# Decoder block with a mixture of experts, one core: half of the experts take 64 tokens, with both weight-side parts of a token in one stationary operand

## The chip, the cores and the metric

One NeuronCore of a Trainium2 chip runs the whole kernel. The metric is the time of one execution in device microseconds (us); the time of a kernel is the median of its runs. TensorE is called PE, VectorE DVE, ScalarE ACT, GpSimd POOL and SyncE SP, as in the profile. A profile comes from one profiled execution, and its span is the time from that execution's first recorded event to its last.

## What is computed

The reference is one decoder layer on 512 tokens of 1024 channels, in float32: a modulated norm, an attention and a delta-rule mixer, a residual, a second modulated norm, and a mixture of experts, of which the change speaks alone:

```python
logits = (xt @ w_router + b_router).astype(jnp.float32)
top_v, top_e = lax.top_k(logits, TOP_K)
gates = jax.nn.softmax(top_v, axis=-1)
...
def clamped_swiglu(hgu):
    gate, up = jnp.split(hgu, 2, axis=-1)
    gate = jnp.minimum(gate, SWIGLU_LIMIT)
    up = jnp.clip(up, -SWIGLU_LIMIT, SWIGLU_LIMIT)
    return gate * jax.nn.sigmoid(SWIGLU_ALPHA * gate) * (up + 1)
...
def expert_block(args):
    xb, e = args
    return clamped_swiglu(xb @ w1[e] + b1[e]) @ w2[e] + b2[e]
```

`w1[e]` is 1024 x 2048 (8 MB), `w2[e]` 1024 x 1024 (4 MB); the output is the residual plus the gated sum of a token's four experts, then a final norm. With the reference's inputs the 32 experts get 20 to 175 tokens: experts 0 and 1 get 23 and 104, the two fullest of the others 175 and 134, the next thirteen 114 to 55, and the last fifteen 49 to 20.

## The kernel before, in words

The first 440 us (mixer, out-projection, router) are not touched. From there the kernel goes through the experts one after the other, 0 to 31 in an order that is made at run time (L1295 to L1324): experts 0 and 1 first, and the two with most tokens at the places H0 = 8 and H1 = 20, where a second list of 128 tokens follows the first. Every other expert has one list of 128 places. A list names the tokens (`idx`) and their gates (`gate`); places that no token fills name a row past the end of the tokens.

A list passes through these steps.
- POOL gathers the tokens' rows from DRAM (`gather`, L1136, tile `xg`). PE transposes them in 8 pieces into PSUM (`transposed`, L1121, tile `tr`); ACT casts them to the fast matmul type float32r (`xH`) and DVE subtracts that from the exact value, which gives the rest (`xL`). A product of two such split numbers takes three matmuls: high by high, high by low, low by high.
- SP loads the weights in tiles of 1 MB (`raw`, twelve in flight). `halves` (L1018) splits half a tile: ACT casts it to `wh` (L1026), and DVE or POOL makes `wl = raw - wh` (L1028). `wh` and `wl` have NS = 4 buffers each, so a split is at most four halves ahead of PE. An expert has 24 halves, 16 of `w1` and 8 of `w2`; a counter over all halves (`hseq`) gives every 12th to POOL (L1027), that is 2 of an expert's 24.
- `up` (L1141): the bias enters PSUM by four matmuls (L1052), and 16 halves follow with six matmuls of 512 columns each (L1151, L1152, L1155). Then ACT computes the Silu (`sg`, L1159), DVE the clamp (L1161, out of PSUM) and the product (L1165).
- `down` (L1168): the result is transposed and split again (`aH`, `aL`), and 8 halves follow with six matmuls each (L1185, L1186, L1189). DVE multiplies by the gate (`y`, L1197), and POOL adds the 128 rows to `yd` in DRAM (L1198); empty places add to spare rows of `yd`.

The steps stand in the order up(i), down(i-1), up(i+1), down(i) (L1372). The transposes are hung in between the tiles of a down projection (`pending`). A scheduler orders each engine's instructions from there; every engine then executes its own in that order. The lists of four experts at a time are made by comparisons on DVE (`oh`, L1091). Rounds that the lists do not hold run in a loop at the end (L1481), as many times as there are such rounds.

```python
1026         S.copy(h, t)
1027         on_g = hseq[0] <= 2 or hseq[0] % 12 == 0 and hseq[0] < 24 * E - 24
1028         sub = (G if on_g else V).tensor_tensor(l, t, h.bitcast(F32), op=OP.subtract)
```

Of the kernel before, what the change touches and what calls it, by code (L numbers as in the profile page):

```python
# [29 lines left out]
Z0, DK0, DQ0, DV0 = 3072, 2048, 1536, 2560  # L30


@with_exitstack
def tile_block(ctx: ExitStack, tc, x, c, w_ada, b_ada, norm1_w, w_in, conv_w, A_log, dt_bias, dn_norm_w,
# [109 lines left out]
    # gates first, every token at once, and the first two heads' keys: their products follow the making of h,  # L144
    # two blocks of channels at a time as the modulation of these is known
# [5 lines left out]
    def modulation(k0, n):  # L151
        """shift1 and scale1 of n blocks of channels; these blocks of h."""
# [64 lines left out]
    def k_split(k):  # L217
        """The lower parts for two blocks."""
# [142 lines left out]
    # every unit of weights is read and split one ahead of its use  # L361
# [6 lines left out]
    def take(n):  # L368
        """The next unit; n pieces of the sums above beside it."""
# [6 lines left out]
    def head(kind, h, wu):  # L376
        """One head's channels: convolution; its tokens on partitions; back to channels. A step per yield."""
# [141 lines left out]
    # (not before the projections are nearly done: the tensor engine goes on with what comes first)  # L519
# [54 lines left out]
    def delta():  # L574
# [121 lines left out]
    def item(p, b, po):  # L696
        """Two heads' queries of a block of tokens; the sums over the keys leave by channel."""
# [53 lines left out]
    def router():  # L751
        """logits = (x1 @ (a2 * w_router)) / rms(x1) + shift2 @ w_router + b_router"""
# [20 lines left out]
    def merge(*gens):  # L773
        """Streams of emission, each with its number of steps, advanced in proportion."""
# [19 lines left out]
    E, H0, H1 = 32, 8, 20  # L794
# [31 lines left out]
    yd = dram.tile([T + P, D], F32, name="yd")  # L826
# [12 lines left out]
    # expert biases: parts of float32r, of b1 on (half, part, expert), of b2 on (part, expert) with the first part again;  # L839
    # 1 comes to the upper half of b1, ALPHA and gate2 to b2  # L840
# [33 lines left out]
    def route_half(b, half, between=lambda: None):  # L874
        """Half of the sum of the squares and of the products with the router."""
# [27 lines left out]
    def top4(b, between=lambda: None):  # L903
# [8 lines left out]
        # top 4 of 32, gates, members  # L912
# [8 lines left out]
    def store(b):  # L921
# [6 lines left out]
        if b == 0:  # L928
            S.dma_start(yd[T:T + P, :], x1b)
# [11 lines left out]
    def place(dst, mk, pp):  # L941
        """Place of every token in the lists; 1024 and more where it is no member."""
# [43 lines left out]
    def init_rec(r):  # L986
        """Tokens as pairs of small numbers, membership, gates."""
# [25 lines left out]
    moe = ctx.enter_context(tc.tile_pool(name="moe", bufs=1, reuse_waits="tile"))  # L1013
    prefetch(NL + 4)
# [3 lines left out]
    def halves(t, j, pin=False):  # L1018
        """The two parts of half of a tile of weights."""
# [23 lines left out]
    def accumulators(n, bsel):  # L1043
        """Of the gate and up projections of one or two lists of tokens, with the biases."""
# [5 lines left out]
        for ac in accs:  # L1050
            for n in range(4):
                PE.matmul(ac[n], bsel(n // 2), b1s[:, (n % 2) * 512:(n % 2) * 512 + 512], start=True, stop=False)  # L1052
# [20 lines left out]
    def gate_parts(r, g):  # L1073
        """A gate as three parts of bfloat16."""
# [5 lines left out]
    def fill_lists(n, pos_of, rec_of, ix, go, gates=None):  # L1080
        """Tokens and gates of n lists; gates: makes these in between."""
        ohs, sl = {}, moe.tile([P, n, 6], F32, name="sl")
        for c0, c1 in ((0, 3), (3, 6)) if gates else ((0, 6),):
# [3 lines left out]
            for i in range(n):  # L1087
                if c0 == 0:
                    oh = ohs[i] = moe.tile([P, NTB, P], BF16, name="oh", bufs=2)
                    for b in range(NTB):  # L1090
                        V.tensor_scalar(oh[:, b], iotaS, pos_of(i, b), None, op0=OP.is_equal)  # L1091
# [10 lines left out]
    # experts 0 and 1 come first: their lists  # L1102
# [11 lines left out]
    i8 = moe.tile([P, 8], U32, name="i8")  # L1114
    ev = moe.tile([P, 2, 3, E], F32, name="ev")
# [5 lines left out]
    def transposed(src, name):  # L1121
# [14 lines left out]
    def gather(e, ix, t):  # L1136
        G.indirect_dma_start(out=t, out_offset=None, in_=h2d,  # L1137
                             in_offset=bass.IndirectOffsetOnAxis(ap=ix, axis=0), bounds_check=T - 1, oob_is_err=False)
        XG[e] = t

    def up(sets, tiles, bsel):  # L1141
        """Gate and up projections of one or two lists of tokens of an expert; clamped SwiGLU."""
        xs = [XT.pop(e) for e, _ in sets]
        pu, p2, accs = ACC.pop() if ACC else accumulators(len(sets), bsel)
        for k, t in enumerate(tiles):
            for j in range(2):
                h, l = PRE.pop(0) if PRE else halves(t, j)
                for (xh, xl), ac in zip(xs, accs):
# [4 lines left out]
                    for n in range(2):  # L1153
                        ns = slice(n * 512, n * 512 + 512)
                        PE.matmul(ac[2 * j + n], xl[:, k], h[:, ns], start=False, stop=(k == KT - 1))  # L1155
        for (e, ut), ac in reversed(list(zip(sets, accs))):
# [11 lines left out]
    def down(sets, tiles, between=lambda i: None, last=False, first=False):  # L1168
        """Down projection, gates, and the sum into the rows of the tokens; sets: key, gates, rows."""
        as_ = [AT.pop(e) for e, _, _ in sets]  # L1170
        if first:
# [6 lines left out]
        for i, t in enumerate(tiles):  # L1178
            for j in range(2):
                h, l = halves(t, j, last and i > 0)  # L1180
                k = 2 * i + j
                for (ah, al), py in zip(as_, accs):
# [7 lines left out]
            if i < 3:  # L1190
                between(i)
        for (_, gcol, ix), py in reversed(list(zip(sets, accs))):
            y = moe.tile([P, D], F32, name="y", bufs=2)
            if last:
                add_rows(y, py, gcol, ix, first)
                continue
            lastv[:] = [V.scalar_tensor_tensor(y, flat(py), gcol, gate2, op0=OP.mult, op1=OP.mult).ins]  # L1197
            G.indirect_dma_start(out=yd, out_offset=bass.IndirectOffsetOnAxis(ap=ix, axis=0), in_=y, in_offset=None,  # L1198
                                 bounds_check=T + P - 1, oob_is_err=True, compute_op=OP.add)

# [1 line left out]
    RES = {}  # L1202

    def residual():
        """What is summed so far, and a place for the result."""
# [9 lines left out]
    def gates_by_expert():  # L1215
        """The parts of the gates: the first twice, the second."""
# [11 lines left out]
    def bias2(pn, b, n):  # L1228
        """The sum of the gates and rows of b2 for half of the channels."""
        PE.matmul(pn, RES["g"][:, b * P:b * P + P], b2s[:96, n * 512:n * 512 + 512], start=True, stop=False)  # L1230

    def add_rows(y, py, gcol, ix, first):
        """Rows of an expert onto the rows of their tokens, by products with zeros and ones; the final norm."""
# [25 lines left out]
        def rms(b, xs):  # L1259
            """The sum of the squares of a block, in one part or two; the scale of its rows."""  # L1260
# [30 lines left out]
    # the first gather goes before the other weights  # L1291
# [7 lines left out]
    r, t, i0, i1, t1, cw = (oe_[:, i] for i in range(6))  # L1299
    m8, hf = oe_[:, 6, 0:8], oe_[:, 7, 0:2]  # L1300
    V.tensor_tensor(cw, pc, tieb, op=OP.add)
    V.max(out=m8, in_=cw)
    V.max_index(out=i8, in_max=m8, in_values=cw)
    V.tensor_copy(hf, i8[:, 0:2])
    V.tensor_scalar(i0, iotaE, hf[:, 0:1], None, op0=OP.is_equal)
    V.tensor_scalar(i1, iotaE, hf[:, 1:2], None, op0=OP.is_equal)
    V.tensor_scalar(t, iotaE, hf[:, 0:1], None, op0=OP.is_gt)
    V.scalar_tensor_tensor(t, iotaE, hf[:, 1:2], t, op0=OP.is_gt, op1=OP.add)
    V.tensor_tensor(r, iotaE, t, op=OP.subtract)
    for h in (H0, H1):  # L1310
        V.scalar_tensor_tensor(r, r, h - 0.5, r, op0=OP.is_gt, op1=OP.add)
    for h, i in ((H0, i0), (H1, i1)):
# [220 lines left out]
```

## Time and profile before

| | |
|---|---|
| time, median of 3 runs | 1752.71 us (1749.81 to 1755.13) |
| the profiled execution, its span | 1756.8 us |
| PE busy in the span | 1636.7 us, 93% |
| DVE busy in the span | 1480.4 us, 84% |
| ACT busy in the span | 1090.4 us, 62% |
| POOL busy in the span | 484.0 us, 28% |
| DMA, mean over the span | 280 GB/s, 491.53 MB |

A busy share is an average over the whole span; the part before 440 us has other limits than the experts. In the timeline a row is a run of like instructions of one engine: start, time to the end of the last, engine, line, operation, output and inputs, how many, and in brackets how long the engine was idle before and who released it. Matmuls are pipelined, so a row of one lasts longer (0.39 us) than the distance to the next (0.23 us).

### The profile page before, as it was taken

The page shows a single profiled execution, that of the slowest core. Times are in us where ns is not written, and L with a number is a line of the kernel's source. Part 1 is how long each engine was busy: PE and PEld are TensorE (multiplying, and loading weights), DVE is VectorE, ACT ScalarE, POOL GpSimd, SP SyncE. Part 2 cuts the span into 40 slices and gives each one's busy share as a digit, 9 for nine tenths or more (in the row PEclk, how much of TensorE's full clock was granted, in tenths as well). Part 3 has the DMA queues.
Part 4 walks back from the last instruction along what each step waited for, and adds up shares of the span by engine and source line. Part 5 has one row for each costly group of instructions (what it writes and reads, how often), then busy time and mean ns, then how long its engine had stood idle before and what let it go on. Part 6 is the DMA issues. An engine that isn't in the chain of part 4 may idle for free.

```text
span 1756.8 us, 23357 instructions
## 1 busy us (share of the span) xinstructions
PE 1636.7 (93%) x8154; PEld 1333.3 (76%) x8154; DVE 1480.4 (84%) x1784; ACT 1090.4 (62%) x1384; POOL 484.0 (28%) x334
## 2 busy tenths in 40 slices
PE   4988989999899999999999999999999999999996
PEld 4767777798687777787777777777777777777774
DVE  6678844667999999949799999999687999999997
ACT  4653223632577777737577677777465777777774
POOL 3426961114232222112123322222122322222111
PEclk7999996999899999999999999999999999999998
DMA  8454551063889999968799999999777999999973
GB/s 267 144 168 139 193 168 49 1 237 154 311 309 337 362 375 374 335 226 299 261 353 365 333 341 356 354 380 352 250 252 273 333 361 369 350 365 342 362 285 109
DMA packets 120409, 491.53 MB, mean 280 GB/s; under 512 B 12727, under 2 KB 40031, under 8 KB 87520
## 3 DMA queue, kind: packets, MB, share of 16 engines
q1 hardware_dynamic: 108528, 459.24, 68.7%
q0 software_dynamic: 10432, 28.06, 7.6%
q10 hardware_dynamic: 1328, 2.70, 0.4%
q8 instruction: 65, 1.06, 0.2%
q14 instruction: 56, 0.46, 0.1%
HBM read 474.32 MB, written 24.65 MB: 284 GB/s over the span
## 4 chain that ended last, share of the span: by engine, by line
PE 58%; DVE 17%; DMA 8%; POOL 6%; issue 6%; ACT 4%; SPq 0%; ACTq 0%; DVEq 0%; POOLq 0%
PE up L1152 10%; PE up L1155 10%; PE up L1151 10%; DVE wl L1028 6%; DMA raw<-in_w 6%; PE py L1185 3%; PE py L1189 3%; PE py L1186 3%; PE tr L1129 2%; POOL blk L496 2%; POOL blk L494 2%; PE up L1052 1%; DVE ut L1161 1%; DVE oh L1091 1%; ACT wh L1026 1%
## 5 line engine op out<-in xcount | busy, mean ns | idle before, releaser
L1026 ACT CAST wh<-raw 128x1024 fp32r<-128x1024 f32 x768 | 802.1, 1051 | 365.2 <-PE up L1155 166.5
L1028 DVE TENSOR_TENSOR wl<-raw,wh 128x1024 fp32r<-128x1024 f32 x705 | 860.9, 1259 | 110.5 <-ACT wh L1026 89.9
L1152 PE MATMUL up<-wl,xH 128*128 128x512 f32 x1024 | 403.2, 394 | 9.5 <-POOL wl L1028 4.9
L1151 PE MATMUL up<-wh,xH 128*128 128x512 f32 x1024 | 401.5, 392 | 0.0
L1155 PE MATMUL up<-wh,xL 128*128 128x512 f32 x1024 | 317.7, 391 | 0.0
L1028 POOL TENSOR_TENSOR wl<-raw,wh 128x1024 fp32r<-128x1024 f32 x63 | 156.7, 2488 | 529.9 <-ACT wh L1026 409.0
L1152 PEld LDWEIGHTS up<-wl,xH 128*128 128x128 f32 x1024 | 193.3, 189 | 58.4 <-DVE wl L1028 10.7
L1155 PEld LDWEIGHTS up<-wh,xL 128*128 128x128 f32 x1024 | 193.0, 189 | 40.7
L1151 PEld LDWEIGHTS up<-wh,xH 128*128 128x128 f32 x1024 | 193.6, 189 | 39.7
L1185 PE MATMUL py<-wh,aH 128*128 128x512 f32 x496 | 203.0, 409 | 0.0
L1186 PE MATMUL py<-wl,aH 128*128 128x512 f32 x496 | 197.0, 397 | 0.0
L1198 POOL DMA_INDIRECT yd<-y,idx x33 | 83.2, 2522 | 343.7 <-ACT wh L1026 168.7
L1189 PE MATMUL py<-wh,aL 128*128 128x512 f32 x496 | 158.2, 398 | 0.0
L1189 PEld LDWEIGHTS py<-wh,aL 128*128 128x128 f32 x496 | 92.8, 188 | 21.4
L1186 PEld LDWEIGHTS py<-wl,aH 128*128 128x128 f32 x496 | 93.5, 188 | 19.0
L1185 PEld LDWEIGHTS py<-wh,aH 128*128 128x128 f32 x496 | 93.5, 188 | 18.6
L1165 DVE SCALAR_TENSOR_TENSOR ut<-sg,ut 128x1024 f32<-128x1024 f32 x32 | 81.6, 2551 | 0.7
L1137 POOL DMA_INDIRECT xg<-h2d,idx x33 | 53.1, 1610 | 76.0 <-PE tr L1129 34.7
L133 ACT CAST wH<-raw 128x1024 fp32r<-128x1024 f32 (+1 forms) x34 | 34.4, 1053 | 54.6 <-DMA raw<-in_w_in 21.2
L354 DVE SCALAR_TENSOR_TENSOR macc<-raw,cond,macc 128x512 f32<-128x512 f32 x62 | 57.0, 959 | 7.9 <-DMA raw<-in_w_ada 7.9
L282 PE MATMUL mm<-hH,wH 128*128 128x512 f32 x144 | 58.6, 407 | 3.5 <-ACT cu L308 1.7
L1129 PE MATMUL tr<-ident,ut 128*128 128x128 f32 x256 | 39.4, 284 | 21.6 <-DVE xL L1131 18.9
(452 smaller groups left out, 2350.3 us busy)
## 6 DMA issues: line engine op xcount, KB each, us to landing
raw<-in_w SPq DMA_DIRECT2D x384, 1024.0 KB, 7.9
raw<-in_w_ada SPq DMA_DIRECT2D x16, 1024.0 KB, 5.0
raw<-in_w_in SPq DMA_DIRECT2D x12, 1024.0 KB, 8.5
raw<-in_w_ada SPq DMA_DIRECT2D x16, 512.0 KB, 9.3
raw<-in_w_out SPq DMA_DIRECT2D x4, 1024.0 KB, 7.8
raw<-in_w_in SPq DMA_DIRECT2D x2, 1040.0 KB
xn<-in_x SPq DMA_DIRECT2D x4, 512.0 KB, 3.9
x<-in_x SPq DMA_DIRECT2D x4, 512.0 KB
```

What stands on the lines that cost most here:

```text
L282: PE.matmul(ps, wh[:, k, js], hH[:, k], start=(k == 0), stop=False)
L1026: S.copy(h, t)
L1028: sub = (G if on_g else V).tensor_tensor(l, t, h.bitcast(F32), op=OP.subtract)
L1129: tc.keep_in_program_order(PE.transpose(pt[:, i], src[:, k * P:(k + 1) * P], ident))
L1151: PE.matmul(ac[2 * j + n], xh[:, k], h[:, ns], start=False, stop=False)
L1152: PE.matmul(ac[2 * j + n], xh[:, k], l[:, ns], start=False, stop=False)
L1155: PE.matmul(ac[2 * j + n], xl[:, k], h[:, ns], start=False, stop=(k == KT - 1))
L1165: lastv[:] = [V.scalar_tensor_tensor(ut, sg, GATE_MAX, ut, op0=OP.min, op1=OP.mult).ins]
L1185: PE.matmul(py[:, n], ah[:, k], h[:, ns], start=(k == 0), stop=False)
L1186: PE.matmul(py[:, n], ah[:, k], l[:, ns], start=False, stop=False)
L1189: PE.matmul(py[:, n], al[:, k], h[:, ns], start=False, stop=(k == KT - 1))
L1198: G.indirect_dma_start(out=yd, out_offset=bass.IndirectOffsetOnAxis(ap=ix, axis=0), in_=y, in_offset=None, bounds_check=T + P - 1, oob_is_ ...
```

## The change

1. The order of the experts is by their number of tokens. The two fullest of experts 2 to 31 go to places 8 and 20, the next thirteen to the even places, the last fifteen to the odd places 3 to 31 (`SMALL`); experts 0 and 1 stay at places 0 and 1. The order is made by comparing every expert with every other on DVE.
2. A list at an odd place holds 64 tokens. Its stationary operand (`hl`) has the high parts of the 64 tokens in columns 0 to 63 and the low parts in columns 64 to 127, so that one matmul with `wh` and one with `wl` give all products, the low parts' in PSUM rows 64 to 127: four matmuls for each half in place of six (`up_small`, and `short` in `down`).
3. The two groups of rows have to be added. ACT copies rows 64 to 127 out of PSUM (`lo`, `ylo`), and matmuls with a 64 x 64 identity add them to rows 0 to 63 (`fold`): four for an up projection, hung into the next down projection, and two for a down projection, after the first tile of the next up projection. Clamp, product and `y` of such a list wait for the fold. The last expert's rows need no fold.
4. Every 4th half of the weights goes to POOL, from half 25 to 743: 6 of an expert's 24 in place of 2.
5. Empty places are no longer scattered: their row is out of bounds and dropped. Gather and scatter of a list of 64 take 64 rows.

Two places in the instruction order. First POOL, in the stretch of ordinary experts after place 20; `wl` is the lower part of half a tile of weights, `xg` the gathered rows, `yd` the sums in DRAM. Before:

```order
L1137 DMA xg_3919<-h2d,idx 128x1024
L1198 DMA yd<-y,idx 640x1024
L1028 TENSOR_TENSOR wl<-raw,wh 128x1024 x2
L1137 DMA xg_3920<-h2d,idx 128x1024
L1198 DMA yd<-y,idx 640x1024
L1028 TENSOR_TENSOR wl<-raw,wh 128x1024 x2
```

And after the change, in the same stretch:

```order
L1158 DMA xg_3924<-h2d,idx 64x1024
L1036 TENSOR_TENSOR wl<-raw,wh 128x1024 x2
L1277 DMA yd<-y,idx 512x1024
L1036 TENSOR_TENSOR wl<-raw,wh 128x1024 x4
L1158 DMA xg_3923<-h2d,idx 128x1024
L1036 TENSOR_TENSOR wl<-raw,wh 128x1024
L1277 DMA yd<-y,idx 512x1024
L1036 TENSOR_TENSOR wl<-raw,wh 128x1024 x5
```

Each list has six subtractions on POOL in place of two, and its gather and its scatter stand among them.

Second DVE, in the same stretch. Before, one list:

```order
L1161 TENSOR_SCALAR ut<-up 128x1024
L1165 SCALAR_TENSOR_TENSOR ut<-sg,ut 128x1024
L1028 TENSOR_TENSOR wl<-raw,wh 128x1024
L1131 TENSOR_TENSOR xL<-tr,xH 128x512 x2
L1028 TENSOR_TENSOR wl<-raw,wh 128x1024 x6
L1131 TENSOR_TENSOR aL<-tr,aH 128x512 x2
L1197 SCALAR_TENSOR_TENSOR y<-py,gate,gate_2011 128x1024
L1028 TENSOR_TENSOR wl<-raw,wh 128x1024 x15
```

After the change, from the clamp of a list of 128 (L1222) to the clamp of the list of 64 that follows (L1194):

```order
L1222 TENSOR_SCALAR ut<-up 128x1024
L1036 TENSOR_TENSOR wl<-raw,wh 128x1024
L1226 SCALAR_TENSOR_TENSOR ut<-sg,ut 128x1024
L1140 TENSOR_TENSOR xH<-tr,xH 128x8x64
L1036 TENSOR_TENSOR wl<-raw,wh 128x1024 x4
L1151 TENSOR_TENSOR aL<-tr,aH 128x512 x2
L1276 SCALAR_TENSOR_TENSOR y<-py,gate,gate_2011 64x1024
L1036 TENSOR_TENSOR wl<-raw,wh 128x1024 x14
L1194 TENSOR_SCALAR ut<-up 64x1024
```

DVE keeps 18 subtractions of a list's 24; `y` and the clamp of the list of 64 (L1276, L1194) stand ahead of later subtractions and read what the fold leaves in PSUM.

The diff, cut to its core:

```diff
+SMALL = frozenset(range(3, 32, 2))
+SLOTS = [8, 20] + [i for i in range(2, 32, 2) if i not in (8, 20)] + sorted(SMALL) + [0, 1]
+ROOM = [64 if i in SMALL else 256 if i in (8, 20) else 128 for i in range(32)]
...
-        on_g = hseq[0] <= 2 or hseq[0] % 12 == 0 and hseq[0] < 24 * E - 24
+        on_g = hseq[0] <= 2 or hseq[0] % 4 == 0 and 24 < hseq[0] < 24 * E - 24
...
+        if half_list:
+            hl = moe.tile([P, KT, 2 * HB], F32R, name=name + "H", bufs=2 if name == "x" else 1)
+            pt = ps2.tile([P, KT, HB], F32, name="tr", bufs=2)
+            for k in range(KT):
+                tc.keep_in_program_order(PE.transpose(pt[:, k], src[:HB, k * P:(k + 1) * P], ident[:HB, :HB]))
+            S.copy(hl[:, :, :HB], pt)
+            V.tensor_tensor(hl[:, :, HB:], pt, hl[:, :, :HB].bitcast(F32), op=OP.subtract)
+            return hl
...
+    def fold(acc, lo, n):
+        for i in range(n):
+            PE.matmul(acc(i), identR[HB:, HB:], lo(i), start=False, stop=True, skip_group_check=True)
+
+    def up_small(e, tiles, bsel):
+        xp = XT.pop(e)
+        pu, _, _ = accumulators(1, None)
+        for k, t in enumerate(tiles):
+            for j in range(2):
+                h, l = halves(t, j)
+                for n in range(2):
+                    ac, ns = pu[:, 2 * j + n], slice(n * 512, n * 512 + 512)
+                    PE.matmul(ac, xp[:, k], h[:, ns], start=(k == 0), stop=False, skip_group_check=True)
...
+                    PE.matmul(ac, xp[:, k], l[:, ns], start=False, stop=(k == KT - 1), skip_group_check=True)
+            if k == 0:
+                while folds:
+                    folds.pop(0)()
+        lo = [moe.tile([P, 1024], F32R, name=n, tag=n) for n in ("ut", "sg")]
+        for j in range(2):
+            S.copy(lo[j][HB:], flat(pu[HB:, 2 * j:2 * j + 2]))
...
+        if short and not last:
+            (_, gcol, ix), py = sets[0], accs[0]
+            lo = moe.tile([P, D], F32R, name="ylo", tag="y")
+            S.copy(lo[HB:], flat(py[HB:]))
+            def rest():
+                fold(lambda i: py[:HB, i], lambda i: lo[HB:, i * 512:i * 512 + 512], 2)
+                add_up(HB, py, gcol, ix)
+            folds.append(rest)
+            return
...
+        G.indirect_dma_start(out=yd, out_offset=bass.IndirectOffsetOnAxis(ap=ix[:n], axis=0), in_=y[:n], in_offset=None,
+                             bounds_check=T - 1, oob_is_err=False, compute_op=OP.add)
...
     V.tensor_tensor(cw, pc, tieb, op=OP.add)
+    V.tensor_tensor(cmp, row(cw), col(cw), op=OP.is_gt)
+    V.tensor_reduce(out=t, in_=cmp, axis=AX.X, op=OP.add)
+    V.tensor_tensor(cmp, row(iotaE), col(t), op=OP.is_equal)
+    V.tensor_tensor(cmp, cmp, row(slots), op=OP.mult)
+    V.tensor_reduce(out=r, in_=cmp, axis=AX.X, op=OP.add)
```

## Rows read from the trace of the kernel before

**Rows 1.** Page, its first line.

```profile
span 1756.8 us, 23357 instructions
```

**Rows 2.** Windows: busy us (instructions) by engine, then PEclk, DMA share, GB/s.

```profile
1465.00:1502.00 37.00, 36.08 (x166) 29.34 (x165) 34.88 (x30) 27.78 (x30) 9.11 (x4) 1.00 0.94 357
747.00:858.00 111.00, 107.50 (x495) 87.36 (x494) 76.80 (x68) 59.66 (x64) 18.30 (x9) 1.00 0.72 259
519.00:1688.00 1169.00, 1130.95 (x5207) 911.03 (x5206) 1056.37 (x1035) 815.20 (x854) 269.86 (x118) 1.00 0.90 334
650.00:675.00 25.00, 24.09 (x113) 19.46 (x112) 23.92 (x22) 18.59 (x21) 5.15 (x3) 1.00 1.00 402
```

**Rows 3.** Timeline, PE: the bias sums that open an up projection.

```profile
519.61 1.09 PE L1052 MATMUL up<-b1s,selp 128*128 128x512 f32 x4
1502.09 1.09 PE L1052 MATMUL up<-b1s,selp 128*128 128x512 f32 x4
1539.48 1.09 PE L1052 MATMUL up<-b1s,selp 128*128 128x512 f32 x4
1687.48 1.09 PE L1052 MATMUL up<-b1s,selp 128*128 128x512 f32 x4
```

**Rows 4.** Timeline, PE: first matmuls of two neighbouring halves, down projection.

```profile
1499.29 0.39 PE L1185 MATMUL py<-wh,aH 128*128 128x512 f32 x1
1500.69 0.39 PE L1185 MATMUL py<-wh,aH 128*128 128x512 f32 x1
```

**Rows 5.** Timeline, ACT: casts of two neighbouring halves, up projection.

```profile
1518.22 1.05 ACT L1026 CAST wh<-raw 128x1024 fp32r<-128x1024 f32 x1 [0.31 <-PE up L1155]
1519.58 1.05 ACT L1026 CAST wh<-raw 128x1024 fp32r<-128x1024 f32 x1 [0.30 <-PE up L1155]
```

**Rows 6.** Timeline, DVE, one list.

```profile
1489.09 1.23 DVE L1161 TENSOR_SCALAR ut<-up 128x1024 f32<-128x1024 f32 x1
1490.35 3.25 DVE L1165 SCALAR_TENSOR_TENSOR ut<-sg,ut 128x1024 f32<-128x1024 f32 x1
1505.51 4.62 DVE L1028 TENSOR_TENSOR wl<-raw,wh 128x1024 fp32r<-128x1024 f32 x4
```

**Rows 7.** Timeline, POOL, the same list.

```profile
1490.12 2.40 POOL L1028 TENSOR_TENSOR wl<-raw,wh 128x1024 fp32r<-128x1024 f32 x1 [14.72 <-ACT wh L1026]
1505.87 2.31 POOL L1198 DMA_INDIRECT yd<-y,idx  x1 [11.32 <-ACT wh L1026]
1509.89 2.51 POOL L1028 TENSOR_TENSOR wl<-raw,wh 128x1024 fp32r<-128x1024 f32 x1 [1.71 <-issue]
```

**Rows 8.** Groups of DVE instructions, 1465 to 1502 us: busy us, mean ns, idle.

```profile
L1028 DVE TENSOR_TENSOR wl<-raw,wh 128x1024 fp32r<-128x1024 f32 x23 | 28.3, 1267 | 2.1 <-ACT wh L1026 1.0
L1131 DVE TENSOR_TENSOR aL<-tr,aH 128x512 fp32r<-128x512 f32 x2 | 1.3, 682 | 0.0
L1197 DVE SCALAR_TENSOR_TENSOR y<-py,gate,gate 128x1024 f32<-128x1024 f32 x1 | 1.3, 1276 | 0.0
```

**Rows 9.** Tile wl, subtractions: ns min/median/max, first and last start.

```profile
L1028 DVE TENSOR_TENSOR wl<-raw,wh x705: 1203/1218/4133, 441.5 to 1730.9; 128x1024 fp32r<-128x1024 f32 x177
L1028 POOL TENSOR_TENSOR wl<-raw,wh x63: 2367/2403/2932, 436.2 to 1675.5; 128x1024 fp32r<-128x1024 f32 x63
```

**Rows 10.** Timeline, tail: DVE sums out of PSUM, POOL product.

```profile
1741.11 2.48 DVE L1275 TENSOR_TENSOR raw<-raw,up 128x512 f32<-128x512 f32 x4 [0.53 <-PE up L1272]
1740.73 2.41 POOL L1277 TENSOR_TENSOR raw<-raw,fnw 128x1024 f32<-128x1024 f32 x1 [14.63 <-DVE raw L1275]
```

**Rows 11.** Page, DMA queues: packets, MB, share of 16 engines.

```profile
q1 hardware_dynamic: 108528, 459.24, 68.7%
q0 software_dynamic: 10432, 28.06, 7.6%
```

**Rows 12.** Timeline, DVE, 463 to 466 us: a comparison and a sum, 512 columns.

```profile
463.15 0.68 DVE L1336 TENSOR_TENSOR o<-tabc,ixf 128x512 f32<-128x512 f32 x1
464.88 1.09 DVE L1339 TENSOR_REDUCE mkb<-o 128x128 bf16<-128x512 f32 x1
```

More of the change, by code (lines that the diff above doesn't have):

```diff
@@ L1049, in accumulators @@
             accs.append([p2[:, 0], p2[:, 1]] + [flat(ps2.tile([P, 4, P], F32, name="tr", bufs=2)) for _ in range(2)])
-        for ac in accs:
-            for n in range(4):
-                PE.matmul(ac[n], bsel(n // 2), b1s[:, (n % 2) * 512:(n % 2) * 512 + 512], start=True, stop=False)
+        if bsel is not None:
+            for ac in accs:
+                for n in range(4):
+                    PE.matmul(ac[n], bsel(n // 2), b1s[:, (n % 2) * 512:(n % 2) * 512 + 512], start=True, stop=False)
         return pu, p2, accs
@@ L1136, in gather @@
     def gather(e, ix, t):
-        G.indirect_dma_start(out=t, out_offset=None, in_=h2d,
-                             in_offset=bass.IndirectOffsetOnAxis(ap=ix, axis=0), bounds_check=T - 1, oob_is_err=False)
+        n = HB if small(e) else P
+        G.indirect_dma_start(out=t[:n], out_offset=None, in_=h2d,
+                             in_offset=bass.IndirectOffsetOnAxis(ap=ix[:n], axis=0), bounds_check=T - 1, oob_is_err=False)
         XG[e] = t
+    folds = []
+    def fold(acc, lo, n):
[11 more added lines that the diff above has]
+                    if k == 0:
+                        PE.matmul(ac[:HB], bsel(j)[:, :HB], b1s[:, ns], start=False, stop=False, skip_group_check=True)
+                    PE.matmul(ac, xp[:, k], l[:, ns], start=False, stop=(k == KT - 1), skip_group_check=True)
+            if k == 0:
+                while folds:
[4 more added lines that the diff above has]
+        def rest():
+            fold(lambda i: pu[:HB, i], lambda i: lo[i // 2][HB:, i % 2 * 512:i % 2 * 512 + 512], 4)
+            sg = moe.tile([P, 1024], F32, name="sg", tag="sg")
+            ut = moe.tile([P, 1024], F32, name="ut", tag="ut")
+            S.activation(sg[:HB], flat(pu[:HB, 0:2]), AF.Silu, scale=ALPHA)
+            V.tensor_scalar(ut[:HB], flat(pu[:HB, 2:4]), -6.0, 8.0, op0=OP.max, op1=OP.min)
+            lastv[:] = [V.scalar_tensor_tensor(ut[:HB], sg[:HB], GATE_MAX, ut[:HB], op0=OP.min, op1=OP.mult).ins]
+            UT[e] = ut
+        return rest
     def up(sets, tiles, bsel):
@@ L1170, in down @@
         as_ = [AT.pop(e) for e, _, _ in sets]
+        short = small(sets[0][0])
         if first:
@@ L1181, in down @@
                 k = 2 * i + j
-                for (ah, al), py in zip(as_, accs):
+                for n in range(2 if short else 0):
+                    ns = slice(n * 512, n * 512 + 512)
+                    PE.matmul(accs[0][:, n], as_[0][:, k], h[:, ns], start=(k == 0), stop=False, skip_group_check=True)
+                    PE.matmul(accs[0][:, n], as_[0][:, k], l[:, ns], start=False, stop=(k == KT - 1), skip_group_check=True)
+                for (ah, al), py in () if short else zip(as_, accs):
                     for n in range(2):
@@ L1324, in tile_block @@
     V.tensor_copy(ei, pi)
-    for i in range(3):
+    for i in range(NR):
         V.tensor_copy(ev[:, 0, i], pi)
-        G.memset(ev[:, 1, i], 128.0 * (i + 1) - 4096.0)
+        V.tensor_scalar(ev[:, 1, i], room, 128.0 * i - 4096.0, None, op0=OP.add)
     oh_f = oh4.rearrange("p b k e -> p (b k) e")
@@ L1353, in make_lists @@
         es = slice(e0, e0 + n)
-        fill_lists(n, lambda i, b: posm[:, b, e0 + i:e0 + i + 1], lambda i, b: rec[:, b, e0 + i], idx[:, es], gate[:, es])
+        fill_lists(n, lambda i, b: posm[:, b, e0 + i:e0 + i + 1], lambda i, b: rec[:, b, e0 + i], idx[:, es], gate[:, es],
+                   places=lambda i: flat(iota64) if small(e0 + i) else iotaS)
     def make_second(i):
@@ L1406, in tile_block @@
         cl = cols_of(i)
-        up([(cl[0], None)] + [(c_, xg[(nx[0] - 1) % 2]) for c_ in cl[1:]], W.pop((1, i)), sel_of(i))
+        if small(i):
+            pending.append(up_small(i, W.pop((1, i)), sel_of(i)))
+        else:
+            up([(cl[0], None)] + [(c_, xg[(nx[0] - 1) % 2]) for c_ in cl[1:]], W.pop((1, i)), sel_of(i))
         for j, col in enumerate(cl):
```

88 lines of the change are left out of this document (42 added, 46 removed).

## The prediction, made before the changed kernel was run

> **What bounds the kernel now.** I read the page first for the span [rows 1], then the windows stage by stage, then the timeline of each engine over one ordinary expert, and last the queues of the DMA. The experts are the place: from the up projection of place 2 to that of place 31 the bias sums stand 1167.9 us apart [rows 3], two thirds of the span. In that stretch PE is busy 1131 us of 1169 and DVE 1056 [rows 2].
>
> One ordinary list takes 37.0 us, as the window of one shows; in it PE is busy 36.1 us, DVE 34.9, ACT 27.8, POOL 9.1, and the DMA engines 94% at 357 GB/s [rows 2]. So three resources lie within 6% of each other, and the one that is eased is not the only one that counts. PE's part is regular: a half of the up projection every 1.36 us, seen in the casts that PE releases [rows 5], a half of the down projection every 1.40 us [rows 4], the bias sums 1.09 us for four [rows 3]; 16 x 1.36 + 8 x 1.40 + 0.9 = 33.9, and the transposes and a short wait make the rest. A second list costs the same again: the window of places 8 and 9 has 111 us for two periods, and DVE is busy only 77 us of it [rows 2]. From rows 3, (1167.9 - 2 x 37) / 29 = 37.7 us for an average list, 0.7 more than an ordinary one, since lists are made beside some. **A pair of lists is 75.5 us before.**
>
> **What the row of the DVE tells.** The product of `sg` and `ut` takes 3.25 us [rows 6]; a subtraction of the same 1024 columns takes 1.22 [rows 9] and `y` 1.28 [rows 8]. What differs is POOL: its subtraction runs from 1490.12 to 1492.52 [rows 7], the product starts at 1490.35 and ends at 1493.60, 1.08 us after POOL's end. It stood still while POOL worked. The longest subtraction on DVE is 4.13 us and the longest on POOL 2.93 [rows 9], so the subtractions block each other too. But four sums that read PSUM ran beside a POOL product of 2.41 us in 2.48 us [rows 10], which is no longer than four such pieces take (0.68 us each [rows 8]), and the clamp, out of PSUM, took 1.23 across POOL's start [rows 6, 7]. So DVE's work between two SBUF tiles and POOL's exclude each other, and DVE's work out of PSUM runs on.
>
> [...]
>
> **The change part by part.**
> - *PE.* A list of 64 has four matmuls for a half in place of six: 24 x 2 = 48 fewer, at 1.40 / 6 = 0.23 us [rows 4] 11.0 us. The fold adds six of 512 columns, 6 x 0.23 = 1.4. So PE needs 37.0 - 9.6 = 27.4 us for a list of 64 and about 37 for one of 128, 64.4 for a pair and 65.8 with the making of lists.
> - *DVE and POOL.* In the window of one list DVE is busy 34.9 us [rows 2]. Of this, 2.0 is the product's wait above, and a subtraction behind the other POOL operation waits between 0 and 2.3; I take half, 1.1. DVE's own work is then 31.7. Four subtractions fewer, at (4.62 - 1.22) / 3 = 1.13 us each in a run of four [rows 6], leave 27.2. A list of 64 saves two more pieces of `xL` and `aL` (they come as one operation of 512 columns in place of two), 1.2 us: 26.0. Against this stand six POOL subtractions a list. Each holds DVE up for 2.26 us if DVE has SBUF work ready (3.25 - 1.22, and the 0.23 by which the product came later than POOL): 6 x 2.26 = 13.6. The sum is 40.8 for a list of 128, 39.6 for one of 64, with 1.5 for the making of lists **81.9 a pair if nothing is hidden**.
> - *What hides.* DVE's readers of PSUM (clamp 1.2, `y` 1.2, four or two pieces at 0.6) are 4.8 and 3.6 us, 8.4 a pair, and can run beside POOL. If all do, DVE needs 73.5, and PE's own 37 + 0.9 for the fold in the list of 128 stands above DVE's 36.0 there: 75.4 a pair. Whether they do is chance: POOL starts when its cast is there, and DVE's order has readers of PSUM at eight places among 36 subtractions. I take half, 77.7.
> - *New waits.* `y` and the clamp of a list of 64 wait on PE for the fold, the one for the first two halves of the next up projection, with DVE's later subtractions queued behind. Between 0 (POOL subtracts in that time) and 3 us a pair (two halves at 0.93, bias and fold); I take 1.3. **79.0 a pair, 3.5 more than before.**
> - *ACT.* Three copies of 1024 columns a pair, some 1 us each by its casts [rows 5], with ACT at 27.8 of 37 us: hidden behind DVE.
> - *DMA.* Scatter and gather are 28 MB in 7.6% of 16 engines' span, 133 us, or 4.0 a list [rows 11]; the empty rows are about half of the scatters. Worth nothing while DVE bounds; it lowers the DMA's share.
> - *Ranking.* Three comparisons and products of 1024 columns and two sums, by 0.68 and 1.09 us for 512 [rows 12] about 8 us on DVE near 450 us, for some 3 us of small operations. Between 0 and 5; I take 3.
> - *The end.* The last 24 halves have no POOL subtraction, and the last list is one of 64: between 0 and 7 us less, I take 3.
>
> **The sum.** Places 2 to 31 are 15 pairs. Where a second list runs, DVE has 34 us to spare in 111 [rows 2], which I count as one pair without loss: 14 x 3.5 = 49, and +3 - 3. On the span of 1756.8 that makes 1806; the median of the runs lies 4.1 below the span, so 1802. [...]
>
> **The rivals.**
> 1. *DVE is relieved* (faster). The six POOL subtractions fall into time in which DVE would wait for casts, its own work falls to 27 us, and PE or the DMA bounds a pair. PE would need 65.8. The weights of a pair, 25.2 MB at the 459 MB in 68.7% of the span of rows 11, take 66.2, with 5.4 for gathers and scatters 71.6; twelve tiles loaded ahead give back 2.1 a pair: 69.5, 6 less than before, 1756.8 - 84 - 4 = 1669. For it: POOL waited 14.7 us for its cast [rows 7], so it is free, and 402 GB/s were seen in one window [rows 2]. Against it: DVE is idle 2.1 us a list [rows 8], and 13.6 us of blocking don't fit there. It decides if DVE's subtractions stay near 1.2 us. 0.13. [...]
> 2. *Break-even.* All readers of PSUM run beside POOL: 75.4 a pair against 75.5, 1740 to 1760. For it: eight places a pair, the longest of them half as long as a POOL operation. Against it: DVE's order is fixed and POOL's operation starts by its own. 0.15.
> 3. *The lists don't hold the tokens*, and rounds run in the loop at the end. A round has nothing to overlap with: 12 tiles at 2.8 us and a list of 37, some 70 us each, 1870 with one on top of my sum. The reference's counts (15 lists of 49 or fewer, 13 of 114 or fewer, 175 and 134 for the two with two lists) speak against it. 0.02.
>
> **How the numbers follow.** My forecast, DVE and POOL in turn as the bound, has 0.70, from 1760 to 1890 as nothing to all but a little is hidden and the new waits cost 3 or 0. What a measurement here can tell from no change is about 0.3%, 1747 to 1758. Faster: rival 1 and a third of rival 2, 0.18. Same: the rest of rival 2, 0.10. Slower: 0.72. The range from 1735 to 1860 leaves out rival 1 and the far end of the forecast.
>
> **What would show it.** Right: bias sums of the odd and the even places some 38 to 40 us apart, 79 a pair; DVE busy over 95% from 520 to 1690 us with its subtractions at a mean near 2 us; some 180 POOL subtractions at 2.4 to 2.9 us; PE idle behind `wl` from DVE and POOL; DMA below 90%. Wrong: subtractions on DVE near 1.2 us beside many on POOL, or odd places near 30 us, or ACT waiting for `raw`. A list of 64 much slower than 40 us would mean that the waits for the fold cost more than I gave them.

## The result, and the profile after

The change makes the kernel slower: 1933.59 us (median of 4 runs, 1923.28 to 1937.38) against 1752.98 us before (4 runs). The ratio is 1.1009, with a 95% interval from 1.0967 to 1.1052. The forecast was 1802, with a range from 1735 to 1860, so the direction was right, and the loss of 181 us is almost four times the 49 that were forecast. The profiled execution took 1934.66 us.

The page of the changed kernel; the first digits row is the clock that PE was granted, in tenths of full speed, over 40 slices of the span, and q1 and q0 are the DMA queues:

```profile
span 1932.9 us, 22209 instructions
...
PE 1618.1 (84%) x7522; PEld 1232.3 (64%) x7522; DVE 1459.8 (76%) x1629; ACT 1103.3 (57%) x1398; POOL 841.9 (44%) x451
...
PEclk7999989998999899999899988889989998888888
...
q1 hardware_dynamic: 108672, 459.28, 65.3%
q0 software_dynamic: 8576, 19.07, 4.5%
```

No engine is full. PE issues 632 matmuls fewer than before (7522 for 8154) and yet is busy for 1618 us against 1637. The bytes of q0 fall from 28.06 to 19.07 MB [rows 11], as the change intends. In the 29 slices from 531 us on, the clock row shows 8 in 14, where [rows 2] had 1.00 in every window.

Windows of the changed kernel, with the columns of [rows 2]: places 2 to 30, the list of place 24 and the list of place 27. A window runs from the bias sums of one list to those of the next, so it holds that list's up projection and most of the down projection of the list before:

```profile
518.00:1854.00 1336.00, 1122.73 (x4614) 824.99 (x4613) 1033.32 (x888) 824.52 (x862) 613.33 (x234) 0.92 0.80 285
1543.00:1580.00 37.00, 33.44 (x143) 24.99 (x143) 34.56 (x23) 25.59 (x26) 20.01 (x8) 0.98 0.86 307
1669.50:1710.50 41.00, 32.92 (x113) 22.19 (x112) 29.99 (x22) 28.79 (x32) 19.62 (x8) 0.83 0.75 266
```

DVE is busy 77% of the stage. The window of place 27 has a fifth fewer matmuls than that of place 24 (113 for 143) and PE is busy for the same 33 us with them, at a granted clock of 0.83.

Timeline of PE: bias sums that open the up projections of places 2, 3, 24, 26, 28 and 31 (as [rows 3]):

```profile
518.13 1.08 PE L1061 MATMUL up<-b1s,selp 128*128 128x512 f32 x4
558.99 0.40 PE L1180 MATMUL up<-b1s,selp 128*64 128x512 f32 x1
...
1543.14 1.10 PE L1061 MATMUL up<-b1s,selp 128*128 128x512 f32 x4
1621.71 0.85 PE L1061 MATMUL up<-b1s,selp 128*128 128x512 f32 x3
1710.53 1.09 PE L1061 MATMUL up<-b1s,selp 128*128 128x512 f32 x4
1853.90 0.63 PE L1180 MATMUL up<-b1s,selp 128*64 128x512 f32 x1
```

Worked as in the prediction, (1853.9 - 518.1 - 2 x 37) / 29 is 43.5 us for a list, 87.0 for a pair, against 75.5 before and a forecast of 79.0. Single pairs differ: places 24 and 25 take 78.6 us, places 26 and 27 take 88.8. Neither is undisturbed: the window of place 24 has a clock of 0.98 and that of place 27 has 0.83. Fourteen and a half pairs by 11.5 us are 167 of the 181.

The tile `wl` of the changed kernel (as [rows 9]):

```profile
L1036 DVE TENSOR_TENSOR wl<-raw,wh x587: 1203/1214/3912, 432.2 to 1905.1; 128x1024 fp32r<-128x1024 f32 x196
L1036 POOL TENSOR_TENSOR wl<-raw,wh x181: 2345/2666/5854, 433.1 to 1864.4; 128x1024 fp32r<-128x1024 f32 x181
```

Over the whole span (busy us, mean ns, then the idle time of DVE before them and who ended it):

```profile
L1036 DVE TENSOR_TENSOR wl<-raw,wh 128x1024 fp32r<-128x1024 f32 x587 | 882.8, 1544 | 249.3 <-ACT wh L1034 246.5
```

The prediction's signs come out mixed. POOL's 181 subtractions, the waits behind `wl` and a DMA below 90% are there. But DVE's subtractions take 1.54 us in the mean, where near 2 was expected, half of them 1.21 or less, and DVE sits idle for 249 us in which it waits for casts.

What PE waited for between 519 and 1890 us (total us, times, longest):

```profile
PE up L1181 <- POOL wl L1036: 71.5, 30, 6.0
PE up L1181 <- DVE wl L1036: 36.5, 23, 2.6
PE py L1247 <- DVE wl L1036: 28.2, 21, 3.9
```

The largest waits fall in the up projection of the lists of 64 (L1181), for POOL's halves, up to 6.0 us at a time. What happens in one of the longest, place 23, is told by the timeline of DVE, POOL, ACT and PE:

```profile
1504.10 6.88 DVE L1036 TENSOR_TENSOR wl<-raw,wh 128x1024 fp32r<-128x1024 f32 x6
1518.85 4.24 DVE L1036 TENSOR_TENSOR wl<-raw,wh 128x1024 fp32r<-128x1024 f32 x3 [7.53 <-ACT wh L1034]
...
1504.45 7.93 POOL L1277 DMA_INDIRECT yd<-y,idx  x1 [2.17 <-DVE y L1276]
1511.92 2.84 POOL L1036 TENSOR_TENSOR wl<-raw,wh 128x1024 fp32r<-128x1024 f32 x1
...
1506.12 3.32 ACT L1034 CAST wh<-raw 128x1024 fp32r<-128x1024 f32 x3 [0.45 <-PE up L1178]
1516.12 1.05 ACT L1034 CAST wh<-raw 128x1024 fp32r<-128x1024 f32 x1 [6.68 <-PE up L1178]
...
1508.43 0.39 PE L1178 MATMUL up<-wh,xH 128*128 128x512 f32 x1
1514.81 0.79 PE L1181 MATMUL up<-wl,xH 128*128 128x512 f32 x1 [5.99 <-POOL wl L1036]
1515.40 0.63 PE L1178 MATMUL up<-wh,xH 128*128 128x512 f32 x1
1515.83 0.63 PE L1181 MATMUL up<-wl,xH 128*128 128x512 f32 x1
```

The scatter starts at 1504.45, 0.35 us after DVE has begun a run of six subtractions with no gap. It ends at 1512.4, 1.4 us after that run, and has taken 7.93 us where the one in [rows 7] took 2.31. Of the 33 scatters eleven take 4.3 to 8.0 us; in the kernel before, three take 5.6 to 6.9. POOL's subtraction stands behind it in POOL's queue, and PE waits 5.99 us for that. ACT waits 6.68 us for PE to free a buffer. DVE, whose run of six is over, has no half to subtract either, and waits 7.53 us for a cast. When PE goes on, its matmuls stand 0.43 us apart (1515.40, 1515.83) and not 0.23. Windows of the same moment show the granted clock:

```profile
1510.20:1513.60 3.40, 0.00 (x0) 0.00 (x0) 1.12 (x3) 0.00 (x0) 3.40 (x2) 0.96 0.33 67
1513.60:1517.00 3.40, 2.19 (x5) 1.81 (x6) 0.00 (x0) 0.88 (x1) 1.15 (x1) 0.50 0.46 90
1517.00:1520.40 3.40, 3.40 (x10) 2.58 (x10) 1.55 (x1) 2.13 (x3) 2.38 (x1) 0.54 1.00 422
```

In the first of these windows PE does nothing. In the second, in which it goes on at 1514.81, its granted clock is 0.50, and in the third, with PE busy throughout, 0.54; from 1520.35 on its matmuls stand 0.23 us apart again. Over the span the granted clock is 0.923, against 0.971 before, where most of the loss lies ahead of the experts: 0.91 up to 519 us, and 1.00 from there to 1688 us [rows 2].

### The profile page after: what moved, and what is told of

The parts are those of the page before. It is cut to its first block, busy times and chain, and to the rows that moved or that the text cites. A ratio compares the mean times of both kernels' runs of the same rounds, so it can differ in the third digit from the quotient of the medians.

```text
span 1932.9 us, 22209 instructions
## 1 busy us (share of the span) xinstructions
PE 1618.1 (84%) x7522; PEld 1232.3 (64%) x7522; DVE 1459.8 (76%) x1629; ACT 1103.3 (57%) x1398; POOL 841.9 (44%) x451
## 3 DMA queue, kind: packets, MB, share of 16 engines
q0 software_dynamic: 8576, 19.07, 4.5%
## 5 line engine op out<-in xcount | busy, mean ns | idle before, releaser
L1036 DVE TENSOR_TENSOR wl<-raw,wh 128x1024 fp32r<-128x1024 f32 x587 | 882.8, 1544 | 249.3 <-ACT wh L1034 246.5
L1034 ACT CAST wh<-raw 128x1024 fp32r<-128x1024 f32 x768 | 786.0, 1049 | 451.2 <-PE up L1213 118.8
L1036 POOL TENSOR_TENSOR wl<-raw,wh 128x1024 fp32r<-128x1024 f32 x181 | 491.9, 2718 | 539.5 <-ACT wh L1034 517.2
L1181 PE MATMUL up<-wl,xH 128*128 128x512 f32 x480 | 221.7, 462 | 108.1 <-POOL wl L1036 71.5
L1210 PE MATMUL up<-wl,xH 128*128 128x512 f32 x544 | 221.0, 406 | 24.5 <-DVE wl L1036 18.3
L1209 PE MATMUL up<-wh,xH 128*128 128x512 f32 x544 | 215.8, 397 | 0.0
L1181 PEld LDWEIGHTS up<-wl,xH 128*128 128x128 f32 x480 | 103.0, 215 | 173.5 <-POOL wl L1036 85.4
L1178 PE MATMUL up<-wh,xH 128*128 128x512 f32 x480 | 209.4, 436 | 2.0 <-ACT wh L1034 2.0
L1277 POOL DMA_INDIRECT yd<-y,idx x33 | 113.1, 3428 | 160.0 <-DVE y L1276 151.1
L1213 PE MATMUL up<-wh,xL 128*128 128x512 f32 x544 | 170.4, 395 | 0.0
L1252 PE MATMUL py<-wl,aH 128*128 128x512 f32 x272 | 118.0, 434 | 24.1 <-DVE wl L1036 20.9
L1247 PE MATMUL py<-wl,aH 128*128 128x512 f32 x224 | 103.2, 461 | 40.6 <-DVE wl L1036 28.2
L1213 PEld LDWEIGHTS up<-wh,xL 128*128 128x128 f32 x544 | 103.2, 190 | 22.3
L1255 PE MATMUL py<-wh,aL 128*128 128x512 f32 x272 | 91.7, 416 | 0.0
```

What stands on the lines that cost most here:

```text
L1178: PE.matmul(ac, xp[:, k], h[:, ns], start=(k == 0), stop=False, skip_group_check=True)
L1181: PE.matmul(ac, xp[:, k], l[:, ns], start=False, stop=(k == KT - 1), skip_group_check=True)
L1209: PE.matmul(ac[2 * j + n], xh[:, k], h[:, ns], start=False, stop=False)
L1210: PE.matmul(ac[2 * j + n], xh[:, k], l[:, ns], start=False, stop=False)
L1247: PE.matmul(accs[0][:, n], as_[0][:, k], l[:, ns], start=False, stop=(k == KT - 1), skip_group_check=True)
L1252: PE.matmul(py[:, n], ah[:, k], l[:, ns], start=False, stop=False)
```

## The experiments

Three theories were tested. **A**: POOL's share makes the loss, since its subtractions and DVE's exclude each other (the prediction's own). **B**: the lists of 64 leave PE pauses, its clock falls, and that makes the loss. **C** (after the first runs): on POOL a subtraction stands behind a scatter that DVE holds up. Ratios are to runs of the kernel before on the same chip, which took 1755.9 to 1757.8 us. The result's chip had 1753.0, so a difference of two medians from different chips can be off by some 5 us.

**The change, POOL's share as before.**

```diff
-        on_g = hseq[0] <= 2 or hseq[0] % 4 == 0 and 24 < hseq[0] < 24 * E - 24
+        on_g = hseq[0] <= 2 or hseq[0] % 12 == 0 and hseq[0] < 24 * E - 24
```

> The change with the share of POOL put back to one subtraction in twelve, as before the change (two a list). Theory A (POOL's subtractions make the loss: they are slow, they stop DVE's, and the next casts wait for the slots they hold): two a list cost what they cost before, the halves of the lists of 64 are cheaper, so about 1740 us (1700 to 1770), and the granted clock is back near 1.00 because nothing makes PE wait. Theory B (the lists of 64 leave PE with too little work, its granted clock falls, and that makes the loss): the clock stays near 0.92 and the time above 1800.

Measured: 1786.13 us, ratio 1.0179 (1.0150 to 1.0208), clock 0.957. Neither theory named this value. Most of the loss goes with the share, but with the share of the kernel before it is still slower than that kernel. In its trace the 28 scatters between 600 and 1650 us take 4.28 us in the mean, and the longest of all 11.13; this is where theory C came from.

**The kernel before, with the change's share.**

```diff
-        on_g = hseq[0] <= 2 or hseq[0] % 12 == 0 and hseq[0] < 24 * E - 24
+        on_g = hseq[0] <= 2 or hseq[0] % 4 == 0 and 24 < hseq[0] < 24 * E - 24
```

> The kernel before, every list of 128, with the change's share alone: one subtraction in four on POOL. A: the waits for POOL's halves come here too, in every list; more than 1850 us. B alone: PE has its six matmuls a half as before, the clock stays at 1.00, and the time stays near 1753.

Measured: 1806.98 us, ratio 1.0292 (1.0258 to 1.0326). Against the kernel before on its own chip the share alone costs 49 us (54 against the 1753 us of the result's chip): the size of the forecast, far below the 100 that A expected when it was asked to explain the whole loss. B alone, with its time near 1753, doesn't hold either. The 27 scatters between 600 and 1650 us take 2.15 us in the mean. The window of this kernel from 519 to 1650 us, and its subtractions on DVE over the whole span:

```profile
519.00:1650.00 1131.00, 1068.24 (x4859) 852.38 (x4858) 952.38 (x864) 756.68 (x791) 516.71 (x222) 0.99 0.88 320
L1028 DVE TENSOR_TENSOR wl<-raw,wh 128x1024 fp32r<-128x1024 f32 x587 | 860.6, 1502 | 187.9 <-ACT wh L1026 180.5
```

PE is busy 94% of this window and DVE 84%. So DVE is not full here either, at a clock of 0.99, though the time is the one that was forecast with DVE as the bound.

**The change with no subtraction on POOL** (`on_g = hseq[0] <= 2`).

> The change with no subtraction on POOL behind the first two. A: nothing blocks DVE; 24 subtractions a list at 1.13 to 1.22 us are 27 to 29 us, with the readers of PSUM 32 to 34 a list, so PE at 37 and DVE at 33 make a pair of 70 to 72, some 1690 us (1670 to 1740). B: 1800 and more, clock below 0.95.

Measured: 1715.73 us, ratio 0.9765 (0.9724 to 0.9807). This lies in A's range, though not at its 1690: without POOL's subtractions the lists of 64 make the kernel no slower. Yet its scatters show C's mechanism at its clearest, timeline of POOL and DVE:

```profile
1177.94 18.08 POOL L1277 DMA_INDIRECT yd<-y,idx  x1 [13.48 <-DVE y L1276]
...
1177.59 17.11 DVE L1036 TENSOR_TENSOR wl<-raw,wh 128x1024 fp32r<-128x1024 f32 x15
1196.50 2.36 DVE L1036 TENSOR_TENSOR wl<-raw,wh 128x1024 fp32r<-128x1024 f32 x2 [1.81 <-ACT wh L1034]
```

DVE subtracts fifteen times in a row, and the scatter ends 1.3 us after the last of them, 18.08 us after its start. No subtraction stands behind it in POOL's queue here.

**The change, with PE kept busy by wide products with zeros.**

```diff
+                    PE.matmul(ac, zr, h[:, ns], start=False, stop=False, skip_group_check=True)
...
+                    PE.matmul(accs[0][:, n], zr, h[:, ns], start=False, stop=False, skip_group_check=True)
```

> The change as it is, with two matmuls of a stationary tile of zeros added to each half of a list of 64, so that PE has six a half in every list and the sums stay what they are. B: PE is kept busy, the granted clock rises above 0.97, and the kernel is faster than the change (1850 or less) although PE does 48 matmuls more a list. A: PE was waiting anyway, so no change (1920 to 1945), or slower where the added 11 us a list of 64 come before the next cast (up to 2000).

Measured: 1839.86 us, ratio 1.0479 (1.0445 to 1.0513), clock 0.969. With 48 matmuls more in each list of 64 it is 94 us faster than the change. B's forecast of the time holds, and its clock is all but reached (0.969 where above 0.97 was expected). Windows of places 24 and 25 of this kernel:

```profile
1500.00:1537.50 37.50, 36.49 (x167) 29.12 (x166) 33.29 (x24) 26.95 (x28) 20.03 (x8) 1.00 0.94 339
1537.50:1577.10 39.60, 38.27 (x171) 29.08 (x170) 34.45 (x26) 30.62 (x33) 23.34 (x8) 1.00 0.92 330
```

At full clock the pair takes 77.1 us.

**The change with the share of before, and without the scatters** (the `indirect_dma_start` of `add_up` left out).

> The change with one subtraction in twelve on POOL (1786 us above) and without the scatters of the lists: the sums are not written out, everything else runs. Theory C (on POOL a subtraction stands in its queue behind a scatter that can't get on while DVE subtracts without a pause; PE waits for that subtraction): the loss of 70 us against no subtractions on POOL goes almost wholly, 1700 to 1730. Theory A (the two subtractions a list cost their own blocking of DVE): 1770 to 1786.

Measured: 1761.08 us, ratio 1.0028 (1.0004 to 1.0052). Between the two: the scatters are 25 of the 70 us that lie between 1786 and 1716, so C is a part of it and not nearly all. The edit takes the scatters' transfers away too, so it doesn't show by itself that their place in POOL's queue is the reason.

**The kernel before with no subtraction on POOL.**

> The kernel before with no subtraction on POOL behind the first two. If the gain of the change without POOL (1716 us) came from the lists of 64, every list here is bound by PE's 36 us and this stays within 1735 to 1755; if it came from leaving POOL alone, this is near 1716 too.

Measured: 1724.25 us, ratio 0.9803 (0.9766 to 0.9840). Of the two cases it is the second, nearly. The interval overlaps that of the change without POOL (0.9724 to 0.9807): most of what that version gains comes from leaving POOL alone, and what the lists of 64 add can't be told from nothing. Its window shows what bounds it, PE full and the DMA at 99%:

```profile
1458.00:1595.00 137.00, 137.00 (x638) 112.75 (x637) 131.69 (x131) 106.31 (x112) 14.94 (x8) 1.00 0.99 370
```

**The kernel before, with PE's work of a list of 64 in every second list.**

```diff
-                    for n in range(2):
+                    for n in range(2 if sets[0][0] not in range(3, 32, 2) or k == KT - 1 else 0):
```

(for the products of `xl`, and likewise for `al`)

> The kernel before, lists all of 128 and POOL's share as it was, with 42 of the 48 matmuls of the lower parts of tokens and activations left out in every second list: PE's work there is that of a list of 64, and nothing else of the change is in it. Theory B: the granted clock falls below 1.00 in those lists and takes back what PE saves, so 1750 to 1790, mean clock below 0.965. Without B: the clock stays at 0.971, DVE bounds, and the time is 1715 to 1750.

Measured: 1763.04 us, ratio 1.0039 (1.0013 to 1.0065), clock 0.959. There are 616 matmuls fewer (7538 for 8154), some 142 us of PE's work at 0.23 us each, and nothing is gained, as B says. DVE at 1012 of 1131 us and the DMA at 91% leave little to gain as well, so this run alone doesn't decide.

**The change with no subtraction on POOL and narrow products with zeros.**

```diff
+                    PE.matmul(ac[:, :128], zr, h[:, n * 512:n * 512 + 128], start=False, stop=False, skip_group_check=True)
...
+                    PE.matmul(accs[0][:, n, :128], zr, h[:, n * 512:n * 512 + 128], start=False, stop=False, skip_group_check=True)
```

> The change with no subtraction on POOL, and with two matmuls of 128 columns with a stationary tile of zeros added to each half of a list of 64 (some 0.06 us each, 3 us a list). If the half-clock stretches that are left there cost time and come from PE's pauses: a higher clock than 0.955 and 1700 us or less. If not: 1716 to 1730, for PE's added work.

Measured: 1703.17 us, ratio 0.9670 (0.9639 to 0.9700), clock 0.966. It is the fastest version found, 3.3% under the kernel before; its interval lies below those of both versions without POOL. It missed the 1700 by 3 us. The window shows what bounds it now, PE full and the DMA too:

```profile
1458.00:1595.00 137.00, 136.48 (x678) 110.03 (x677) 133.06 (x130) 114.98 (x118) 43.94 (x7) 1.00 0.99 380
```

**The change with the same narrow products** (its share of POOL kept).

> The change as it is, with two matmuls of 128 columns and a stationary tile of zeros added to each half of a list of 64 (some 0.06 us each at full clock, 3 us a list), between the products of the upper and of the lower part, where PE waits for the lower part. They take too little of PE's time to set the pace of the halves, as the wide ones (1840 us above) might have. Theory B: the granted clock rises from 0.923 to 0.95 or more, and the time falls to 1890 or less. If the wide ones helped by their pace and not by the clock: 1920 to 1950.

Measured: 1872.86 us, ratio 1.0666 (1.0636 to 1.0697), clock 0.943. It is 61 us faster than the change with some 3 us a list more to do (48 matmuls at a quarter of 0.23 us, an estimate from their columns), so the wide products did not help by their pace alone, and the clock rose with the gain. The clock came back less far than I expected (0.95).

**The change without the scatters** (its share kept).

> The change with its own share of POOL and without the scatters of the lists, so that the sums are not written out. Theory C: POOL's subtractions no longer stand behind scatters of 4 to 8 us in the lists of 128's sums, so PE pauses less and the clock comes back in part: 1880 or less. If the scatters matter little at this share: 1915 to 1940.

Measured: 1889.04 us, ratio 1.0754 (1.0708 to 1.0800), clock 0.930. The scatters are worth 45 us; the expectation missed by 9.

**The kernel before with the change's share, and PE's work of a list of 64 in every second list** (the edits of the second and the seventh run together).

> The kernel before with one subtraction in four on POOL (1807 us above) and with 42 of the 48 matmuls of the lower parts left out in every second list. It does the same work as that kernel on every engine but PE, and 42 matmuls, some 10 us, less on PE in a list. Theory B: the pauses that this makes on PE lower its clock, and with less to do the kernel is slower than with all its products: 1820 to 1900, clock below 0.95. Without B: not above 1807.

Measured: 1891.48 us, ratio 1.0748 (1.0704 to 1.0791), clock 0.934. This is the run that decides for B's first half, that PE's saved work turns against the kernel: no fold, no list of 64, no other scatter, only fewer matmuls than the 1807 us kernel, and it is 84 us slower. Its window, beside the one of the second run above:

```profile
519.00:1650.00 1131.00, 969.82 (x4058) 738.38 (x4057) 944.05 (x823) 694.36 (x740) 495.39 (x207) 0.94 0.84 299
```

In the same 1131 us PE gets through 4058 matmuls and DVE through 823 instructions, where the second run has 4859 and 864; the clock is 0.94 against 0.99. PE's waits for `wl`, of this run (519 to 1800 us) and then of the second (519 to 1740 us):

```profile
PE up L1152 <- DVE wl L1028: 90.2, 43, 4.6
...
PE py L1186 <- DVE wl L1028: 27.8, 25, 2.1
...
PE up L1152 <- DVE wl L1028: 3.7, 3, 3.3
```

In the up projection PE waits 90.2 us for DVE's lower parts, where the second run has 3.7. How much of the 84 us is the clock itself can be bounded. The mean clock is 0.934 over 1890.9 us here and 0.968 over 1806.4 there, so by (1 - clock) x span some 125 and 58 us of PE's full-clock time were not granted. The 67 us more are the most that the clock itself can have cost (an estimate from these means). The rest of the 84 is not assigned; DVE's instructions also got longer, 1.15 us in the mean of the window (944.05 / 823) where the second run has 1.10 (952.38 / 864). The same bound for the narrow products of the ninth run gives 43 of their 61 us.

**The change with the wide products and without the scatters.**

> The change with the wide products with zeros in the lists of 64 (1840 us above) and without the scatters of the lists, so that the sums are not written out. If the loss has three parts that add up, the share of POOL 54 us, the clock 84 and the scatters in front of POOL's subtractions 45, then only the share is left: 1795 to 1815, as the kernel before with that share. If the scatters cost only through the clock, which the wide products have brought back already: 1830 to 1845.

Measured: 1820.72 us, ratio 1.0359 (1.0321 to 1.0397), clock 0.965. Between the two again: once PE is kept busy, the scatters are worth 19 us and not 45. So about half of their cost is gone where PE is kept busy.

## Why the prediction was wrong

**The size of the share's price came out, and partly by luck.** The forecast of 79.0 us a pair was 3.5 above before, 49 us in all, and the share alone costs 49. But not in the way that was forecast. By the prediction's prices DVE works 38.4 us in a list of 128 (40.8, less half of 4.8 hidden) and is the bound. In the second run it is busy 84% of some 39 us, 33 a list, and else waits for casts. Less 27.2 of its own work and some 0.75 for the making of lists, that leaves about 0.9 us of blocking for each POOL subtraction, where 1.9 was charged (2.26 with the hidden half taken off). Idle time that the prediction did not charge made up for it: before its subtractions DVE idles 188 us in the second run, mostly for casts, and 110 in the kernel before. What sets the period there, with PE at 94% and DVE at 84%, no run separates. POOL's instructions came as counted, 181 at a median of 2.67 us.

**The step that failed is the first one, "PE needs 37.0 - 9.6 = 27.4 us for a list of 64".** It counted PE's saved time as slack, worth nothing but also costing nothing, and the sum has no term for the clock, which [rows 2] show at 1.00. The slack is not free. By the prediction's own prices PE has work for 4 x 0.93 = 3.7 us in the time that POOL and DVE need for four halves, 2.26 + 3 x 1.13 = 5.65 us if they exclude each other, so by these it pauses again and again. With the pause of place 23 ACT waited 6.68 us for PE to free a buffer and DVE, of the forecast bound, 7.53 us for a cast; after it the granted clock was 0.50 and PE's matmuls stood 0.43 us apart. The eleventh run against the second puts the pauses with all that follows at 84 us, of which the lower clock itself can be 67 at most. DVE, forecast above 95%, is at 77%; it had 84% in the second run, so the pauses explain only the part below that.

**The second is "Worth nothing while DVE bounds", of the scatters.** The prediction costed their bytes and left out their place in POOL's queue. With six subtractions a list, one nearly always stands close behind a scatter, and at place 23 a scatter that met a run of six of DVE's subtractions held that one up: it took 7.93 us where the one in [rows 7] took 2.31. The tenth run puts the scatters at 45 us; the twelfth, with PE kept busy, at 19. Both runs also lack the scatters' transfers, so that the queue is the reason is read from the timeline and not shown by a run of its own.

Each taken against the kernel before on its own chip, the share is 49 us, PE's pauses 86 and the scatters 48. They make 183 us where 181 were measured, if the folds and the rest are worth nothing together. The twelfth run says that the parts are not independent, so the close sum is in part luck, an account and not a proof of each size.

**The small terms.** The ranking was put at +3: the bias sums of place 2 start at 518.13, 1.5 us earlier than in [rows 3]. The end was put at 3 us less: from the bias sums of place 31 to the end of the span it is 79.0 us against 69.3, so 9.7 more. The waits for the folds were put at 1.3 us a pair. Between 519 and 1890 us DVE is idle for 28.5 us before `y` and 18.4 before the clamps of the lists of 64, at most 3.1 a pair, and not all of it for folds: 8.4 of it is for an earlier scatter. With the wide products it is 20.6 us in the twelve pairs between 600 and 1650 us, 1.7 a pair. So the term was small, as forecast, and its size is not shown.

**The rivals.** Rival 1, DVE relieved, didn't happen: it needed POOL's subtractions to cost DVE nothing. Nor did rival 2, the break-even: the share alone costs 2.9%. Rival 1's floor was the right thing to look at all the same: without POOL the lists run against PE and a DMA at 97 to 99% and 370 to 380 GB/s, and the gain ends there, at 1703 us in the best version. Rival 3 is out too: no round ran in the loop (33 gathers and 33 scatters, as before). A rival in which PE's saving turns against the kernel was not among the three.

**What stays open.** How a scatter slips through a run of DVE's work in one case (2.31 us in [rows 7], beside four subtractions in [rows 6]) and not in another was not settled, nor was the part of the 84 us that the clock itself can't explain. More than four buffers for `wh` and `wl`, which would let the casts run further ahead of a late half, were not tried.

## What to carry to other kernels

The time taken off PE, which was nearly full, turned into pauses, and with all that follows these cost 84 us in the eleventh run: price the granted clock as a term of its own, and ask of each saving on PE whether what feeds it gets faster too. Before work is moved to POOL, look at what it stands behind in POOL's queue, the scatters above all. And try the opposite of the change's sharing: without subtractions on POOL the kernel before is 2.0% faster, and with the lists of 64 and a little filling work on PE 3.3%.

## What the runs showed of the hardware that was not expected

Less work made a kernel slower: 42 matmuls fewer in every second list, 1807 to 1891 us, with nothing else changed. And work that adds only zeros made one faster, 1934 to 1840 us.

A scatter on POOL took 18.08 us while DVE ran fifteen subtractions without a gap, and ended 1.3 us after the last of them, so the two did not take turns instruction by instruction there. The scatter in [rows 7] took 2.31 us. That it waited for DVE is read from these times; what in it waits, no run here shows.
